# Low-rank branches of a hybrid DiT block: inner weights folded into the in-projection columns on the chip

## Chip, cores and metric

One core of a Trainium2 chip runs the whole program in one launch. The metric is the device time of one execution in microseconds (us). All matrix products are float32 made of three float32r passes: each operand is split into a high part (rounded to float32r) and a low part (what is left), and a product is low x high + high x low + high x high.

## The reference, cut to what matters

The input has 1024 latent tokens ("x") and 256 context tokens ("c"), 1024 wide. An even layer is followed by an odd one. In the odd layer the normed tokens h are multiplied by `in_o`; its first 512 columns give u. u goes through a token shift and then through small inner weights: two of rank 32 for the decay, two of rank 32 for the rate, one of width 96 for the gate:

```python
def token_shift_mix(z, mu):
    zp = jnp.pad(z, ((0, 0), (1, 1), (0, 0)))
    nb = 0.5 * (zp[:, :-2] + zp[:, 2:])
    return z + (nb - z) * mu
...
uw, ua, ugt = (token_shift_mix(u, mu[i]) for i in (3, 4, 5))
g = jax.nn.sigmoid(ugt @ g1) @ g2
tanh(uw @ w1[d]) @ w2[d]        # decay, d = 0, 1
(ua @ a1[d]) @ a2[d]            # rate, d = 0, 1
```

The shift is linear, so the token's own share is u times ((1 - mu) * l1) and its neighbours' share is u times (mu/2 * l1), where l1 = [w1[0], w1[1], a1[0], a1[1], g1] is 512 x 224. u itself is used for nothing else.

## The kernel before, in words

Tokens lie along the free axis, channels on the partitions. A token block is 512 x-tokens (`XB`, two of them) or the 256 context tokens (`CB`). A dense product (`dense`, L294 to L306) goes by output tiles of 128 channels and by token blocks: 24 matmuls (8 channel tiles of the input by three passes) into one of four PSUM banks (`d`), which a consumer then empties.

The order of every engine's instructions is the order in which the code is written. Weights come through `wstream` (L236): one raw buffer `wr` takes a 512 KB tile by a DMA of SyncE, ScalarE casts it to the high half `wh` (L267), GpSimd subtracts to the low half `wl` (L268), and only then may the next tile be loaded to `wr`. SyncE issues its DMAs in the order of the code, and one that has to wait holds back all behind it.

The stretch around the change, in order:

1. The even layer's output projection, tiles m = 0 to 7 of `out_e` (weights 24 to 31 of the stream). For m = 0 to 3 all three token blocks, for m = 4 to 7 x0 and c (first pass), then x1 for m = 4 to 7 (second pass). `fin` (L789) empties the bank on VectorE into the residual `x2x`/`x2c`, ScalarE squares it (L798), GpSimd adds it to `accx`/`accc` (L799). During m = 3 the weights `w2` (tile `rows`) become `WS`: a ScalarE cast (L823) and a VectorE subtraction (L824).
2. The norm of each token block (`norm1`): a ones-matmul (L312) of the sums, an inverse root, and `norm_apply` (L391 to L410) by channel tile over VectorE, ScalarE and GpSimd. Block x0 is done beside the second pass, c after it, x1 beside the next step.
3. u for 4 tiles (weights 32 to 35) and all blocks: 4 x 3 products of 24 matmuls, each emptied by a cast on ScalarE (L847) and a subtraction on VectorE (L848). In between `lora_weights` (L890) makes l1 times (1 - mu) and l1 times mu/2: 24 small VectorE products (L901), two casts, two GpSimd subtractions.
4. `stage1` in `odd_in` (L935 to L960): u by the own and by the neighbour weights, 12 matmuls each, for the 128 decay and rate columns (tile 0, all blocks) and the 96 gate columns padded to 128 (tile 1, x blocks). The neighbours' result `LB` is added shifted to `LA` by GpSimd (L957) and VectorE (L958).
5. The gate's second product (L1393), the projections of k, v and r (L1018) and everything after.

From step 5 on both kernels hold the same instructions in the same order on every engine.

Of the kernel before, what the change touches and what calls it, by code (L numbers as in the profile page):

```python
# [8 lines left out]
F32 = mybir.dt.float32  # L9
F32R = mybir.dt.float32r  # L10
# [169 lines left out]
class Kern:  # L180
# [56 lines left out]
    def wstream(self):  # L237
# [4 lines left out]
        order += [A["in_o"][m] for m in range(4)]  # L242
# [16 lines left out]
        def load(i):  # L259
            raws[i] = self.wfirst = self.wp.tile([128, 8, 128], F32, tag="wr", name="wr")  # L260
            self.wload(raws[i], order[i] if i < n else rest[0])

        def split(i):
            p = self.extra.get(i) or (self.wp, self.wpb)[(n - i) % 2]
# [5 lines left out]
        self.load, self.after = load, None  # L270
# [152 lines left out]
    def layer_even(self, es):  # L423
# [339 lines left out]
        self.WS = self.s_lpw.enter_context(tc.tile_pool(name="lpw", bufs=1)).tile([96, 4, DB], F32R, name="WS")  # L763
        s_x1 = ExitStack()
# [6 lines left out]
        rp0 = s_x0.enter_context(tc.tile_pool(name="rp0", bufs=1))  # L771
        xn, accs, store = {}, {}, []

        def fetch_x(m):
            for s, c0, n in BLK:
                x = (rp1 if c0 else rp0).tile([128, n], F32, tag=f"x2{s}{m}", name=f"x2{s}{m}")
# [8 lines left out]
        def fin(m):  # L785
            def f(s, c0, n, ps):
# [6 lines left out]
                if m == 0:  # L793
                    accs[s, c0] = (rp1 if c0 else rp0).tile([128, n], F32, tag=f"acc{s}", name=f"acc{s}")
# [16 lines left out]
        rows = rp0.tile([96, 4, DB], F32, name="rows")  # L811
        for i in range(3):
            nc.sync.dma_start(out=rows[32 * i:32 * i + 32], in_=A["w2"].rearrange("(g p) n -> p g n", p=32))
        ws = {}
        for m in range(8):
# [6 lines left out]
            if m == 3:  # L822
                nc.scalar.copy(self.WS, rows)  # L823
                nc.vector.tensor_tensor(out=self.WS[32:64], in0=rows[32:64], in1=self.WS[32:64].bitcast(F32), op=ALU.subtract)  # L824
        for m in range(4, 8):
# [6 lines left out]
            if m == 6:  # L832
                w = [next(self.wit)]
# [6 lines left out]
        self.s_up = ExitStack()  # L840
        up = self.s_up.enter_context(tc.tile_pool(name="up", bufs=1))
        self.U = U = [[up.tile([128, TT], F32R, name=f"u{b}{k}") for k in range(4)] for b in range(2)]

        def ue(k):
            def f(src, c0, n, ps):
                o = c0 + (0 if src == "x" else T)
                nc.scalar.copy(U[0][k][:, o:o + n], ps)  # L847
                nc.vector.tensor_tensor(out=U[1][k][:, o:o + n], in0=ps, in1=U[0][k][:, o:o + n].bitcast(F32), op=ALU.subtract)  # L848
            return f
        w.append(next(self.wit))  # L850
        n = 0
        for _ in self.dense(w[0], rhs, XB[:1], ue(0)):
            n += 1
            if n == 18:
                norm = norm1(XB[1])
                next(norm)
        for k, blocks in ((1, XB[:1]), (0, CB), (1, CB), (2, XB[:1] + CB), (0, second), (1, second), (2, second)):
            if k == len(w):
                w.append(next(self.wit))
            if blocks is second and k == 0:  # L860
                list(norm)
            for _ in self.dense(w[k], rhs, blocks, ue(k)):
                n += 1
                if n % self.PN1 == 0:
                    next(norm, None)
            if blocks is second and k == 0:
                s_x1.close()
                self.lora_weights()
        for _ in self.dense(next(self.wit), rhs, BLK, ue(3)):
            pass  # L870
        s_wq.close()
        for k in range(8):
# [16 lines left out]
    def lora_weights(self):  # L889

        tc, nc, A, hmu, omu = self.tc, self.nc, self.A, self.hmu, self.omu
        up = self.s_up.enter_context(tc.tile_pool(name="ul", bufs=1))
        l1 = up.tile([128, 4, 224], F32, name="l1")
        nc.sync.dma_start(out=l1, in_=A["l1"])
        self.LS = LS = []
        for i, mcol in ((0, omu), (1, hmu)):
            lw = up.tile([128, 4, 256], F32, tag="lw", name="lw")
            nc.gpsimd.memset(lw, 0.0)
            for k in range(4):
                for mi, c0, n in ((3, 0, 64), (4, 64, 64), (5, 128, 96)):  # L900
# [1532 lines left out]
```

## Time and profile before

| | us |
|---|---|
| median of the runs | 1514.9 (1507.59 to 1519.34, 3 runs) |
| the profiled execution | 1519.35 |
| its span in the trace | 1517.6 |
| TensorE busy / VectorE / GpSimd / ScalarE | 1366.9 / 987.0 / 679.3 / 639.3 |
| mean granted TensorE clock, share of full | 0.957 |

The span is what the trace covers; 1.75 us lie around it. A busy TensorE is not TensorE at its peak: what counts for a change is how far apart its matmuls start, and where it stands still.

### The profile page before, as it was taken

The numbers are of one execution on the slowest core, as the hardware profiler recorded it, in microseconds if no ns is written. First come the engines' busy times: TensorE is split into PE (matmuls) and PEld (weight loads), VectorE is DVE, ScalarE is ACT, GpSimd is POOL, SyncE is SP. The second block draws the span as 40 slices with busy tenths as digits, with TensorE's granted clock in tenths as the row PEclk, the third lists the DMA queues.
The fourth block names the chain that finished last, engine by engine and source line by source line (L and its number), as shares of the span: only waits on it lengthen the run. The fifth ranks groups of instructions, "written<-read, shape, count | busy, mean of one in ns | idle before, by whom it ended". The sixth has DMA issues, their size and how long they took to land.

```text
span 1517.6 us, 32067 instructions
## 1 busy us (share of the span) xinstructions
PE 1366.9 (90%) x12820; PEld 1074.3 (71%) x12820; DVE 987.0 (65%) x1679; ACT 639.3 (42%) x1259; POOL 679.3 (45%) x943
## 2 busy tenths in 40 slices
PE   6799999999999999898799887698998888887996
PEld 1478888888888778676677666576776666765675
DVE  3745655436711651269999973688668788678756
ACT  2551212121312543456566431243546554566634
POOL 1344535457545441135554540766564665433003
PEclk9999999999999999999899998898999999888998
DMA  8424544453154211536667687555656666755323
GB/s 267 157 81 147 166 156 170 152 167 139 49 170 142 77 41 33 149 101 198 197 196 221 199 277 189 144 135 148 178 138 167 186 163 152 248 167 143 119 81 111
DMA packets 163941, 232.30 MB, mean 153 GB/s; under 512 B 26352, under 2 KB 119920, under 8 KB 163664
## 3 DMA queue, kind: packets, MB, share of 16 engines
q1 hardware_dynamic: 162496, 228.68, 49.9%
q8 instruction: 101, 1.65, 0.5%
q10 hardware_dynamic: 1296, 1.57, 0.3%
q14 instruction: 48, 0.39, 0.1%
HBM read 164.93 MB, written 63.31 MB: 150 GB/s over the span
## 4 chain that ended last, share of the span: by engine, by line
PE 55%; DVE 20%; DMA 8%; issue 5%; POOL 5%; ACT 5%; SPq 2%; DVEq 0%; ACTq 0%; POOLq 0%
PE d L302 28%; PE d L1970 5%; PE d L1018 4%; PE d L2112 3%; PE sc L1534 2%; PE d L946 2%; POOL tmp L1434 2%; POOL X L1435 2%; DMA Bc<-ED 1%; DVE acc L1991 1%; PE pa L1751 1%; PE d L2317 1%; DMA ad<-in_ada_e 1%; PE pa L1756 1%; PE pa L1775 1%
## 5 line engine op out<-in xcount | busy, mean ns | idle before, releaser
L302 PE MATMUL d<-sx,wh 128*128 128x512 f32 x1152 | 361.7, 395 | 3.0 <-DVE sx L528 1.9
L302 PEld LDWEIGHTS d<-sx,wh 128*128 128x128 f32 x1152 | 217.3, 189 | 53.9 <-DVE sx L528 2.4
L302 PE MATMUL d<-sx,wl 128*128 128x512 f32 x576 | 230.1, 399 | 4.5 <-DVE u L848 2.7
L1434 POOL TENSOR_TENSOR tmp<-X,Bc 128x120 f32<-128x120 f32 (+2 forms) x300 | 124.4, 415 | 148.5 <-DMA Bc<-ED 126.2
L268 POOL TENSOR_TENSOR wl<-wr,wh 128x1024 fp32r<-128x1024 f32 x37 | 94.0, 2540 | 190.6 <-ACT wh L267 181.1
L1018 PE MATMUL d<-sx,wh 128*128 128x512 f32 x512 | 162.7, 399 | 0.0
L1970 PE MATMUL d<-sx,wh 128*128 128x512 f32 x384 | 138.4, 431 | 0.0
L1435 POOL TENSOR_TENSOR X<-X,tmp 128x120 f32<-128x120 f32 (+2 forms) x300 | 122.8, 409 | 23.5
L302 PEld LDWEIGHTS d<-sx,wl 128*128 128x128 f32 x576 | 109.0, 189 | 29.6 <-issue 3.3
L629 DVE SCALAR_TENSOR_TENSOR junk<-wra,cb 128x1024 bf16<-128x1024 f32 x56 | 101.1, 1805 | 30.3 <-DMA wra<-in_ada_o 17.5
L1018 PEld LDWEIGHTS d<-sx,wh 128*128 128x128 f32 x512 | 98.7, 193 | 22.1 <-issue 2.4
L1018 PE MATMUL d<-sx,wl 128*128 128x512 f32 x256 | 111.4, 435 | 0.0
L302 PE MATMUL d<-sc,wh 128*128 128x256 f32 x576 | 104.1, 281 | 0.0
L302 PEld LDWEIGHTS d<-sc,wh 128*128 128x128 f32 x576 | 88.8, 190 | 1.4
L1991 DVE SCALAR_TENSOR_TENSOR acc<-hc,vec,acc 128x960 f32<-128x960 f32 (+14 forms) x120 | 88.0, 761 | 1.0
L267 ACT CAST wh<-wr 128x1024 fp32r<-128x1024 f32 x37 | 38.7, 1045 | 112.3 <-PE d L302 82.8
L1970 PEld LDWEIGHTS d<-sx,wh 128*128 128x128 f32 x384 | 73.8, 199 | 16.4
L1970 PE MATMUL d<-sx,wl 128*128 128x512 f32 x192 | 82.7, 430 | 2.7 <-POOL wl L1944 2.7
L302 PE MATMUL d<-sc,wl 128*128 128x256 f32 x288 | 81.0, 281 | 0.0
L1224 POOL TENSOR_TENSOR kd<-kd,Z 128x512 f32<-128x512 f32 x20 | 29.9, 1497 | 75.5 <-DVE kd L1220 75.5
L1534 PE MATMUL sc<-w,bk 64*128 64x128 f32 (+1 forms) x640 | 51.5, 302 | 8.1 <-DMA bk<-BKD 8.1
L1018 PEld LDWEIGHTS d<-sx,wl 128*128 128x128 f32 x256 | 49.3, 193 | 11.6 <-issue 1.9
(382 smaller groups left out, 2889.2 us busy)
## 6 DMA issues: line engine op xcount, KB each, us to landing
wr<-in_in_o SPq DMA_DIRECT2D x32, 512.0 KB
wr<-in_in_e SPq DMA_DIRECT2D x24, 512.0 KB
wra<-in_ada_o SPq DMA_DIRECT2D x24, 512.0 KB
BKD<-bk SPq DMA_DIRECT2D x40, 256.0 KB
BTD<-X SPq DMA_DIRECT2D x20, 512.0 KB
bk<-BKD SPq DMA_DIRECT2D x40, 256.0 KB
Bc<-ED SPq DMA_DIRECT2D x20, 512.0 KB
bkt<-BTD SPq DMA_DIRECT2D x40, 256.0 KB
```

The source lines that it names most:

```text
L267: self.nc.scalar.copy(hi, raw)
L268: self.nc.gpsimd.tensor_tensor(out=lo, in0=raw, in1=hi.bitcast(F32), op=ALU.subtract)
L302: self.nc.tensor.matmul(ps[:, :n], lhsT=w[a][:, k, :], rhs=rhs(src, k, b, c0, n), start=(i == 0), stop=(i == len(seq) - 1))
L629: nc.vector.scalar_tensor_tensor(out=junk, in0=w, scalar=1.0, in1=cb[:, s, :], op0=ALU.mult, op1=ALU.mult, accum_out=dst[:, s:s + 1])
L946: nc.tensor.matmul(ps[:, :n], lhsT=LS[which][a][:, k, 128 * mt:128 * mt + 128], rhs=U[b][k][:, o:o + n], start=(i == 0), stop=(i == len(se ...
L1018: nc.tensor.matmul(ps, lhsT=w[a][:, k, :], rhs=rhs(s, k, b, c0, m), start=(q == 0), stop=(q == len(seq) - 1))
L1434: g.tensor_tensor(out=t, in0=X[:, :, j:j + 1].to_broadcast([128, 8, m]), in1=B[:, j, :, j + 1:16] if j < 8 else B2[:, j - 8, :, j - 7:8], ...
L1435: g.tensor_tensor(out=X[:, :, j + 1:16], in0=X[:, :, j + 1:16], in1=t, op=ALU.add)
L1534: nc.tensor.matmul(ps[h][:, d, i, h:h + 1] if ctx else ps[h][:, d, i], lhsT=bk[R[h], c, d, i], rhs=w[R[h], c, d, sl, i, :], start=True, st ...
L1970: nc.tensor.matmul(ps, lhsT=wt(a, k), rhs=rhs("x", k, b, c0, 512), start=(i == 0), stop=(i == len(seq) - 1))
L1991: nc.vector.scalar_tensor_tensor(out=acc[:, o], in0=hc[:, q], scalar=w, in1=acc[:, o], op0=ALU.mult, op1=ALU.add)
L2112: nc.tensor.matmul(ps, lhsT=wt(a, at), rhs=ysrc(k, b, c0), start=(i == 0), stop=(i == len(seq) - 1))
```

## The change

u is no longer computed. The chip multiplies the in-projection columns of u by the two sets of inner weights first: M = in_o[:, :512] times [(1 - mu) l1, mu/2 l1], 1024 x 448, and then multiplies the tokens h by M. For that:

- The four tiles of the stream that held in-projection columns (weights 32 to 35) are read from a transposed copy `in_oT` of the same numbers, so that u's channels lie on the partitions. `in_oT` is laid out on the host beside the other weights.
- `LA` (the results of both tiles) and `LB` (one neighbour buffer) get a place for the whole stretch, and are used before as landing places: `w2` is loaded to `LA`, l1 to `LB`. Both loads move from the start of the output projection to m = 2.
- `lora_weights` moves to m = 4 of the first pass, behind `WS`. Each of its 24 pieces is now a product (high half) and a scalar_tensor_tensor (low half), both on VectorE.
- Weight 34 is loaded to `LB` as soon as l1 has been read from there, by a DMA written in front of the fetch of the residual for m = 6. Weight 35 is loaded and split early as well, so that all four are there when M starts.
- M is made in two halves of four channel tiles, each 48 matmuls of 448 columns into all four banks `d`, emptied by four casts (ScalarE) and four subtractions (VectorE). In half 1 the four weights are the outer loop, in half 2 the inner one. The norm of c is written in front of half 1, the start of the norm of x1 between the halves.
- `branch` multiplies the tokens by M: 8 channel tiles x 3 passes for (tile, own or neighbour) and block, in the order x0 (4 products), c (2), x1 (4). Tile 1 is 96 wide, no longer padded.
- Context and x0 residual tiles get pools apart (`rpc`, `rp0`).

The core of the diff:

```diff
-        order += [A["in_o"][m] for m in range(4)]
+        order += [A["in_oT"][m] for m in range(4)]
...
+        self.LA = LA = la.tile([128, 2, TT], F32, name="LA")
+        LB = [la.tile([128, TT + 3], F32, name="LB")]
...
-            if m == 3:
+            if m == 2:
+                nc.sync.dma_start(out=l1, in_=A["l1"])
+                for i in range(3):
+                    nc.sync.dma_start(out=rows[32 * i:32 * i + 32], in_=A["w2"].rearrange("(g p) n -> p g n", p=32))
+            if m == 4:
                 nc.scalar.copy(self.WS, rows)
                 nc.vector.tensor_tensor(out=self.WS[32:64], in0=rows[32:64], in1=self.WS[32:64].bitcast(F32), op=ALU.subtract)
+                LW = self.lora_weights(lwp, l1)
+
+                self.raws[34] = LB[0][:, 0:1024].rearrange("p (a n) -> p a n", a=8)
+                self.wload(self.raws[34], self.order[34])
...
-            if m == 6:
-                w = [next(self.wit)]
+            if m == 4:
+                self.split(34)
+            else:
+                w.append(next(self.wit))
+            if m == 5:
+                self.load(35)
+            elif m == 6:
+                self.split(35)
+        self.after()
+        self.after = None
+        w.append(self.ready[35])
         keep()
         list(norm1(first[1]))
...
+        M = [up.tile([128, 8, 448], F32R, name=f"M{b}") for b in range(2)]
+        for hf in range(2):
+            sums = [self.psd.tile([128, 512], F32, tag="d", name="d")[:, :448] for _ in range(4)]
+            for m, q in ([(m, q) for m in range(4) for q in range(4)], [(m, q) for q in range(4) for m in range(4)])[hf]:
+                for e, (a, b) in enumerate(((1, 0), (0, 1), (0, 0))):
+                    nc.tensor.matmul(sums[q], lhsT=w[m][a][:, 4 * hf + q, :], rhs=LW[b][:, m, :], start=(m + e == 0), stop=(m + e == 5))
+            for q, ps in enumerate(sums):
+                hi, lo = (M[b][:, 4 * hf + q, :] for b in range(2))
+                nc.scalar.copy(hi, ps)
+                nc.vector.tensor_tensor(out=lo, in0=ps, in1=hi.bitcast(F32), op=ALU.subtract)
+            if hf == 0:
                 norm = norm1(XB[1])
                 next(norm)
...
+            seq = [(k, a, b) for k in range(KD) for a, b in ((1, 0), (0, 1), (0, 0))]
+            for i, (k, a, b) in enumerate(seq):
+                nc.tensor.matmul(ps, lhsT=M[a][:, k, o:o + p], rhs=rhs(s, k, b, c0, n), start=(i == 0), stop=(i == len(seq) - 1))
...
+        for b, mts in ((XB[0], (1, 0)), (CB[0], (0,))):
+            for mt in mts:
+                for q in (1, 0):
+                    for _ in branch(mt, q, b):
...
+                    nc.vector.tensor_scalar(out=h, in0=l1[:, k, c0:c0 + n], scalar1=m, scalar2=None, op0=ALU.mult)
+                    nc.vector.scalar_tensor_tensor(out=l, in0=l1[:, k, c0:c0 + n], scalar=m, in1=h.bitcast(F32), op0=ALU.mult, op1=ALU.subtract)
```

Three places show how instructions move. First SyncE's queue in the last part of the first pass, before: `wr_3462` is weight 31, the last of `out_e`, and `x2x6` the residual for m = 6.

```order
L294 DMA wr_3391<-in_out_e 128x1024
L783 DMA XR_83<-x2x3_3152 128x512
L777 DMA x2x6_3427<-in_xT 128x512
L777 DMA x2x6_3429<-in_xT 128x512
L777 DMA x2c6_3431<-in_ctxT 128x256
L294 DMA wr_3462<-in_out_e 128x1024
```

The same place now, with `wr_3524` for weight 31:

```order
L298 DMA wr_3400<-in_out_e 128x1024
L796 DMA XR_83<-x2x3_3159 128x512
L298 DMA LB_2936<-in_in_oT 128x1024
L790 DMA x2x6_3489<-in_xT 128x512
L790 DMA x2x6_3491<-in_xT 128x512
L790 DMA x2c6_3493<-in_ctxT 128x256
L298 DMA wr_3524<-in_out_e 128x1024
```

The load of weight 34 to `LB` stands in front of the residual for m = 6 and of weight 31.

Second VectorE at the same time, now; `x2c4` is the last bank emptied for m = 4, `x2x5` the first for m = 5, and between the two parts 42 more rows alternate in the same way.

```order
L802 SCALAR_TENSOR_TENSOR x2c4_3268<-d_3402,mode_115,x2c4_3268 128x256
L841 TENSOR_TENSOR WS_2928<-LA_2935,WS_2928 32x2048
L966 TENSOR_SCALAR LH_3434<-LB_2936,omu_100 128x64
L967 SCALAR_TENSOR_TENSOR LL_3435<-LB_2936,omu_100,LH_3434 128x64
...
L966 TENSOR_SCALAR LH_3434<-LB_2936,hmu_99 128x64
L967 SCALAR_TENSOR_TENSOR LL_3435<-LB_2936,hmu_99,LH_3434 128x64
L966 TENSOR_SCALAR LH_3434<-LB_2936,hmu_99 128x96
L967 SCALAR_TENSOR_TENSOR LL_3435<-LB_2936,hmu_99,LH_3434 128x96
L802 SCALAR_TENSOR_TENSOR x2x5_3365<-d_3495,mode_115,x2x5_3365 128x512
```

Before, `x2x5` followed `x2c4` directly, and `WS` stood one bank earlier; 48 small instructions on `LB` are new here.

Third GpSimd at the end of the second pass, before: the sums for m = 4 to 7 and, as `wl_3760`, the split of weight 33.

```order
L799 TENSOR_TENSOR accx_3045<-accx_3045,sq_3698 128x512
L799 TENSOR_TENSOR accx_3045<-accx_3045,sq_3727 128x512
L799 TENSOR_TENSOR accx_3045<-accx_3045,sq_3756 128x512
L268 TENSOR_TENSOR wl_3760<-wr_3598,wh_3759 128x1024
L799 TENSOR_TENSOR accx_3045<-accx_3045,sq_3789 128x512
L398 TENSOR_TENSOR sc11_136<-x2c1_2959,sc10_135 128x256
```

Now, with the splits of weights 34 (`wl_3764`), 33 (`wl_3797`) and 35 (`wl_3832`):

```order
L812 TENSOR_TENSOR accx_3052<-accx_3052,sq_3760 128x512
L272 TENSOR_TENSOR wl_3764<-LB_2936,wh_3763 128x1024
L812 TENSOR_TENSOR accx_3052<-accx_3052,sq_3793 128x512
L272 TENSOR_TENSOR wl_3797<-wr_3660,wh_3796 128x1024
L812 TENSOR_TENSOR accx_3052<-accx_3052,sq_3828 128x512
L272 TENSOR_TENSOR wl_3832<-wr_3800,wh_3831 128x1024
L812 TENSOR_TENSOR accx_3052<-accx_3052,sq_3861 128x512
L402 TENSOR_TENSOR sc11_136<-x2c1_2966,sc10_135 128x256
```

Two more splits stand among the sums, in front of the norm of c (`sc11`).

## Rows read from the trace of the kernel before

**Rows 1.** The page: busy time by engine, and the chain that ended last.
```profile
PE 1366.9 (90%) x12820; PEld 1074.3 (71%) x12820; DVE 987.0 (65%) x1679; ACT 639.3 (42%) x1259; POOL 679.3 (45%) x943
...
PE 55%; DVE 20%; DMA 8%; issue 5%; POOL 5%; ACT 5%; SPq 2%; DVEq 0%; ACTq 0%; POOLq 0%
```
**Rows 2.** Timeline of TensorE, end of the first pass: start us, us, what.
```profile
471.18 0.39 PE L302 MATMUL d<-sx,wl 128*128 128x512 f32 x1
...
476.78 0.28 PE L302 MATMUL d<-sc,wl 128*128 128x256 f32 x1
...
479.65 0.40 PE L302 MATMUL d<-sx,wl 128*128 128x512 f32 x1
...
488.12 0.40 PE L302 MATMUL d<-sx,wl 128*128 128x512 f32 x1
```
**Rows 3.** Timeline of TensorE, u and stage1; brackets: idle before, and releaser.
```profile
519.98 0.58 PE L302 MATMUL d<-sx,wl 128*128 128x512 f32 x1
...
541.12 0.77 PE L302 MATMUL d<-sx,wl 128*128 128x512 f32 x1 [2.66 <-DVE u L848]
...
544.78 0.40 PE L302 MATMUL d<-sx,wl 128*128 128x512 f32 x1
...
582.91 0.47 PE L946 MATMUL d<-u,LL 128*128 128x512 f32 x1 [0.97 <-POOL LB L939]
...
607.66 1.02 PE L1393 MATMUL d<-LA,g 96*128 96x512 f32 x2
```
**Rows 4.** Stretches: us, busy PE, PEld, DVE, ACT, POOL (instructions), granted clock, DMA share, GB/s.
```profile
472.00:474.00 2.00, 2.00 (x11) 1.58 (x10) 0.00 (x0) 0.38 (x1) 0.94 (x2) 1.00 0.90 219
474.00:476.00 2.00, 2.00 (x10) 1.63 (x9) 0.00 (x0) 0.94 (x1) 0.00 (x0) 1.00 1.03 398
540.00:545.00 5.00, 3.88 (x10) 3.11 (x11) 4.59 (x6) 3.52 (x7) 1.66 (x1) 0.66 0.00 0
```
**Rows 5.** Timeline of VectorE: WS, the last bank of m = 4.
```profile
466.40 2.28 DVE L824 TENSOR_TENSOR WS<-rows,WS 32x2048 fp32r<-32x2048 f32 x1 [2.56 <-ACT WS L823]
...
471.38 0.48 DVE L789 SCALAR_TENSOR_TENSOR x2c<-d,mode,x2c 128x256 f32<-128x256 f32 x1 [1.92 <-PE d L302]
```
**Rows 6.** Line 901 by itself: duration ns min/median/max, first and last start.
```profile
L901 DVE TENSOR_SCALAR lw<-l,omu x12: 247/248/264, 561.4 to 563.3; 128x64 f32<-128x64 f32 x8, 128x96 f32<-128x96 f32 x4
```
**Rows 7.** Timeline of ScalarE: WS, squares, casts of weights, start of c's norm.
```profile
464.47 1.90 ACT L823 CAST WS<-rows 96x2048 fp32r<-96x2048 f32 x1
...
471.96 0.42 ACT L798 ACTIVATE sq<-x2c 128x256 f32<-128x256 f32 x1 [1.77 <-DVE x2c L789]
...
482.30 1.05 ACT L267 CAST wh<-wr 128x1024 fp32r<-128x1024 f32 x1 [1.46 <-DMA wr<-in_out_e]
...
521.33 0.46 ACT L376 ACTIVATE rs<-a,cstt 128x256 f32<-128x256 f32 x1
```
**Rows 8.** Timeline of SyncE's queue: issues at m = 6 of the first pass.
```profile
478.61 0.33 SPq L294 DMA_DIRECT2D wr<-in_out_e  x1
...
479.46 0.95 SPq L777 DMA_DIRECT2D x2x<-in_xT  x2
480.46 0.50 SPq L777 DMA_DIRECT2D x2c<-in_ctxT  x1
```
**Rows 9.** Timeline of GpSimd: x0's norm, sums, a weight's split, end of c's norm.
```profile
506.52 1.87 POOL L398 TENSOR_TENSOR sx<-x2x,sx 128x512 fp32r<-128x512 f32 x1 [7.93 <-ACT sx L406]
...
516.68 4.05 POOL L799 TENSOR_TENSOR accx<-accx,sq 128x512 f32<-128x512 f32 x3 [0.31 <-ACT sq L798]
520.69 2.41 POOL L268 TENSOR_TENSOR wl<-wr,wh 128x1024 fp32r<-128x1024 f32 x1
...
532.11 0.74 POOL L398 TENSOR_TENSOR sc<-x2c,sc 128x256 fp32r<-128x256 f32 x1 [0.51 <-ACT sc L406]
```
**Rows 10.** Timeline of VectorE: two of the norm's subtractions (L400).
```profile
505.17 0.75 DVE L400 SCALAR_TENSOR_TENSOR sx<-x2x,modo,sx 128x512 fp32r<-128x512 f32 x1
...
507.38 1.57 DVE L400 SCALAR_TENSOR_TENSOR sx<-x2x,modo,sx 128x512 fp32r<-128x512 f32 x1
```

More of the change, by code (lines that the diff above doesn't have):

```diff
@@ L268, in split @@
             self.nc.gpsimd.tensor_tensor(out=lo, in0=raw, in1=hi.bitcast(F32), op=ALU.subtract)
-        self.load, self.after = load, None
+        self.load, self.split, self.after = load, split, None
         load(0)
@@ L810, in layer_even @@
         fetch_x(0)
-        rows = rp0.tile([96, 4, DB], F32, name="rows")
-        for i in range(3):
-            nc.sync.dma_start(out=rows[32 * i:32 * i + 32], in_=A["w2"].rearrange("(g p) n -> p g n", p=32))
+        rows = LA[0:96].rearrange("p a t -> p (a t)")[:, 0:4 * DB].rearrange("p (g n) -> p g n", g=4)
+        l1 = LB[0][:, 0:896].rearrange("p (k n) -> p k n", k=4)
         ws = {}
@@ L855, in layer_even @@
                 norm = norm1(XB[1])
                 next(norm)
[L857 to L868, printed above, removed]
@@ L869, in layer_even, with branch @@
-        for _ in self.dense(next(self.wit), rhs, BLK, ue(3)):
-            pass
+        next(self.wit)
+        LB.append(lwp.tile([128, TT + 3], F32, tag="lwh", name="LB1"))
+        for b in LB:
+            for c in (0, T + 1, TT + 2):
+                nc.gpsimd.memset(b[:, c:c + 1], 0.0)
+        def branch(mt, q, b):
+            s, c0, n = b
+            p, o = (128, 96)[mt], 224 * q + 128 * mt
+            ps = self.psd.tile([128, 512], F32, tag="d", name="d")[0:p, :n]
+            seq = [(k, a, b) for k in range(KD) for a, b in ((1, 0), (0, 1), (0, 0))]
+            for i, (k, a, b) in enumerate(seq):
+                nc.tensor.matmul(ps, lhsT=M[a][:, k, o:o + p], rhs=rhs(s, k, b, c0, n), start=(i == 0), stop=(i == len(seq) - 1))
+                yield 1
+            z = c0 + (0 if s == "x" else T)
+            if q:
+                z += 1 if s == "x" else 2
+                nc.scalar.copy(LB[mt][0:p, z:z + n], ps)
+            else:
+                nc.scalar.copy(LA[0:p, mt, z:z + n], ps)
+            if self.after:
+                self.after()
+                self.after = None
@@ L871, in layer_even @@
+        list(norm)
+        s_x1.close()
+        for mt in (1, 0):
+            for q in (1, 0):
+                for _ in branch(mt, q, XB[1]):
+                    pass
+            shifted(mt)
+            if mt:
+                Hg = LA[0:96, 1, 0:T]
+                nc.scalar.activation(out=Hg, in_=Hg, func=AF.Tanh, scale=0.5)
+                nc.vector.tensor_scalar(out=Hg, in0=Hg, scalar1=0.5, scalar2=0.5, op0=ALU.mult, op1=ALU.add)
+        s_up.close()
         s_wq.close()
+        s_lw.close()
```

100 lines of the change are left out of this document (36 added, 64 removed).

## The prediction

> **What bounds the kernel now.** I read the page first: TensorE is busy for 90% of the span, and the chain that ended last runs through it for 55% [rows 1]. So a shorter stretch of matmuls shortens the program, provided that nothing TensorE waits for becomes later. Both kernels hold the same instructions in the same order from the gate's second product on, so the question is only when TensorE gets there. I then read TensorE's timeline from the end of the first pass to that point. A block of 24 matmuls of 512 columns takes 476.78 - 471.18 = 5.60 us, one of 256 columns 479.65 - 476.78 = 2.87 us [rows 2]. u starts at 519.98 and the gate's product at 607.66 [rows 3], 87.7 us later. In that stretch TensorE hardly rests: it waits 2.66 us for a bank that VectorE empties late, and 0.97 us at the change of PSUM pools [rows 3]. In the five microseconds around the first wait the granted clock averages 0.66, against 1.00 in the other two stretches shown [rows 4], so part of it ran on the lower level, 1.2 GHz. Last I followed the other queues (SyncE, VectorE, ScalarE, GpSimd), because the change puts new work and a new wait in each.
>
> **Matmuls.** Before: u is 8 blocks of 512 and 4 of 256; stage1 is 96 matmuls of 512, as many as 4 blocks, and 24 of 256, 1 block. 12 x 5.60 + 5 x 2.87 = 81.6 us. After: branch is 8 blocks of 512 and 2 of 256. M is 96 matmuls of 448 columns, 4 blocks; no row has that width, and it lies between 2.87 and 5.60. The line through both gives 2.87 + 192/256 x 2.73 = 4.92 us. 8 x 5.60 + 2 x 2.87 + 4 x 4.92 = 70.2 us. **-11.3 us.** (With M's blocks at 5.60, their upper end, -8.6.)
>
> **Old waits.** Between 541.12 and 544.78 nine matmuls started [rows 3], 3.66 us for what takes 9 x 0.233 = 2.10 at the full clock: 1.56 us lost to the lower level. The wait of 2.66 and this loss go, since u's banks go: **-4.2 us**. The wait at the change of pools moves behind branch and stays.
>
> **Weight 31 comes late.** This is the first new wait, and the change does not show it as one. Weight 34 may not land in `LB` before l1 has been read there, so its DMA waits for the last of the 48 small VectorE instructions. SyncE issues in order, and behind that DMA stand the residual for m = 6 and weight 31, which m = 7 multiplies by from 488.12 on [rows 2]. The steps: the last bank of m = 4 is empty at 471.86 [rows 5]; its square ends at 472.38; the cast of WS takes 1.90, to 474.28 [rows 7]; the subtraction of WS 2.28, to 476.6 [rows 5]. A product of that size lasts 248 ns and, where nothing holds it, starts 0.17 us after the one before [rows 6]. Here the second of each pair reads what the first wrote, so it starts after the first's end. I take 0.28 for the first and 0.19 for the second, 0.47 a pair, an estimate near the full duration: 24 pairs are 11.3 us, to 487.9. (If the pairs overlap like the rows, 24 x 0.35 = 8.4; with no overlap, 24 x 0.50 = 12.) From weight 34's issue to weight 31's, SyncE needs some 0.4 + 1.0 + 0.5 = 1.9 us [rows 8]: weight 31 is issued at 489.8 instead of 478.61. Alone it landed 3.7 us later, at 482.30 [rows 7, 8]. Now 1.15 MB are on the way in front of it; at the best rate of the rows, 398 GB/s [rows 4], these and its own 0.52 MB take 4.2 us from about 490, so it lands near 494.4. The cast of 1.05 [rows 7] and the split of 2.41 [rows 9] end at 498.0. TensorE stands still from 488.12: **+9.9 us**. The ends: with 8.4 for the pairs and a landing after 3.7 it is 6.2. Upwards, GpSimd splits weight 30 just then, and VectorE and GpSimd hold each other up: beside a GpSimd instruction of 1.87 us [rows 9] a VectorE subtraction took 1.57 instead of 0.75 [rows 10]. One such loss of 0.8, or one of a whole split, 2.4, and DMAs at 219 GB/s [rows 4] (3.4 more) make 15.8. After the wait the clock is low for a while, as above: **+1.5**. The banks cost nothing meanwhile: m = 5's are emptied by 489, and m = 6 needs two others.
>
> On the loss between VectorE and GpSimd the Trainium skill (SBUF — State Buffer, section "SBUF: two separate sides") goes further than the row: a VectorE instruction with two SBUF inputs, or in a two-port mode, and a GpSimd instruction exclude each other for the whole instruction. By that rule VectorE waits for all of weight 30's split, and the term is 9.9 + 2.4 = 12.3 instead of 9.9. The rows show only a collision with a shorter instruction, so I keep 9.9.
>
> **M waits three times.** Call E the end of the second pass, where u starts before (519.98 [rows 3]). GpSimd now does sum, split 34, sum, split 33: from 516.68 [rows 9] that is 2 x 1.35 + 2 x 2.41 = 7.5 us, to E + 4.2; half 1 reaches weight 33 after its first quarter, at E + 2.5, and waits 1.7. Only then is `wr` free for weight 35: landing 3.7 later, cast 1.05, split 2.41, E + 11.5; half 1 gets there at E + 9.1 and waits 2.4. It ends near E + 14.0. All four banks are then full, and their casts stand on ScalarE behind c's norm, which stands behind the cast of weight 35 and one more square (E + 9.7). Before, that norm took from 521.33 [rows 7] to 532.85 [rows 9], 11.5 us: to E + 21.2. Cast and subtraction of the first bank take some 1.2 us; half 2 starts at E + 22.4 instead of E + 14.0. The waits: 1.7 + 2.4 + 8.4 = **+12.5 us**, and **+1.5** for the clock behind the longest. From below: 6, if c's norm keeps to its bare durations and only the banks are waited for. From above: 15 and two such losses of the clock. The rest of x1's norm fits beside branch on x0 and c, 4 x 5.60 + 2 x 2.87 = 28 us.
>
> **Free edits.** The padding of tile 1 costs columns of weights only, and the matmuls go by tokens: nothing. The earlier loads of l1 and `w2` have three output tiles to land in. The zero fill, casts and splits of l1 that go lay beside u's matmuls: nothing.
>
> **Sum.** -11.3 - 4.2 + 9.9 + 1.5 + 12.5 + 1.5 = +9.9 us. On the profiled execution that is 1519.35 + 10 = 1529. That execution was 4.4 us above the median of the runs, so against the median I say 1514.9 + 9.9 = 1525. With all low ends, -15.5 + 6.2 + 1.5 + 6 + 1.5 = -0.3; with all high ones, and M's blocks at 5.60, -12.8 + 15.8 + 1.5 + 15 + 3 = +22.5.
>
> **Rivals.**
> *Weight 31 is in time.* If SyncE does not stand at weight 34 (the pairs quicker than any row, or the wait met earlier), the terms 9.9 and 1.5 go: 9.9 - 11.4 = -1.5, 1513. Against it: the order of SyncE's queue and 48 instructions behind WS. For it: I have no row of these pairs. Part of it counts here too, anything between -10 and 0.
> *The whole gain arrives.* Both new waits are hidden: -15.5, 1499. Against it speak both chains above; for it only that each rests on estimated overlaps.
> *The clock stays low through M.* Three waits in some 30 us, one long stop just before. If the clock does not come back between them, M's 96 matmuls run at 3.66/2.10 = 1.74 times the time: 19.7 becomes 34.3, +14.6 in place of 1.5, and the sum is +23: 1538. It decides as soon as half 1 and half 2 both run on the lower level. For it: one wait of 2.66 was enough to bring the level down [rows 3, 4]. Against it: it was back within four microseconds. The Trainium skill (TensorE: Matmul & The Clock Gate, section "HAM oscillation — how this bites in real kernels") tells of a kernel in which every group of matmuls starts on the lower level because each is preceded by a wait; the row shows one wait alone, and so decides neither way.
>
> **How the numbers follow.** The forecast has 0.55, weight 31 in time 0.25, the low clock through M 0.15, the whole gain 0.05. A measurement of this kernel can tell about 1% (15 us) from no change. The forecast and the first rival lie within it: same 0.80. The third is beyond: slower 0.15. The second sits at the edge: faster 0.05. The forecast's own range goes from about 0 to +15, 1515 to 1530; to hold 8 in 10 with the first rival's lower part, the upper ends, and runs that differ by several microseconds, the range is 1508 to 1534.
>
> **What would show it.** In the profile of the changed kernel: the DMA `LB<-in_in_oT` issued near 488 and weight 31 near 490; a wait of TensorE for `wl` by GpSimd near 488 to 498, in front of m = 7; M's rows 0.2 us apart; waits of some 2, 2 and 8 us inside M, the last for VectorE's `M`; granted clock below 1 behind the longest waits; everything from the gate's product on as before, only shifted. The prediction is wrong if m = 7 starts on time, if half 2 follows half 1 without a wait, or if the shift at the gate's product is not the change of the whole.

## The result, and the profile after

The changed kernel takes 1527.2 us (median of 21 runs, 1520.8 to 1537.7) beside 1514.9 us for the kernel before (21 runs on the same chip): ratio 1.0078, 95% interval 1.0057 to 1.0099. That is 12.4 us or 0.8% slower: within the 1% that the prediction called no change, and inside its range. The profiled execution took 1529.83 us with a span of 1528.0; the span of before was 1517.6. A ratio, here and in the table below, is taken over the runs within 1.5% of the fastest run of their kernel; this leaves out few, but a run of l1_apart that took 4354.9 us, and five of the twelve runs of full, where a single run of 1486.7 us sets the bar.

The page, busy time by engine and the chain that ended last, now:

```profile
PE 1360.9 (89%) x12748; PEld 1065.2 (70%) x12748; DVE 999.0 (65%) x1699; ACT 634.7 (42%) x1253; POOL 670.2 (44%) x939
...
PE 29%; DVE 14%; issue 6%; DMA 6%; POOL 3%; ACT 3%; SPq 1%; DVEq 0%; ACTq 0%; POOLq 0%
```

TensorE is busy 6 us less than in [rows 1], and the program is longer: matmuls were saved, and waits took more than they gave. The second line does not show that. Its shares add up to 62% of the span, because the chain is followed back only to 561.50, inside M; so its 29% for TensorE cannot be set beside the 55% of [rows 1]. TensorE's timeline shows the waits; first the end of the first pass (start, duration, what; in brackets idle time before and its releaser), which answers to [rows 2]:

```profile
480.22 0.28 PE L306 MATMUL d<-sc,wl 128*128 128x256 f32 x1
...
488.68 0.28 PE L306 MATMUL d<-sc,wl 128*128 128x256 f32 x1
...
505.57 0.79 PE L306 MATMUL d<-sx,wl 128*128 128x512 f32 x1 [13.93 <-POOL wl L272]
...
513.56 0.28 PE L306 MATMUL d<-sc,wl 128*128 128x256 f32 x1
```

This execution is 3.44 us late already in the c block of m = 5 (480.22 against 476.78 [rows 2]); it has been since 73 us, in the loads at the start, which the change does not touch. So stretches are compared, not clock times. From that c block to the gate's product it was 607.66 - 476.78 = 130.9 us [rows 2, 3] and is 624.06 - 480.22 = 143.8: **+13.0**, about the change of the whole. The first part of it is the 13.93 in front of m = 7, which was due 2.87 us behind the c block of m = 6 (488.68). That block of 24 then takes 513.56 - 505.57 = 7.99 instead of 5.60: 2.4 lost to the lower clock. The second part is in M (answers to [rows 3]):

```profile
539.76 0.55 PE L878 MATMUL d<-LH,wl 128*128 128x448 f32 x1
540.16 0.37 PE L878 MATMUL d<-LL,wh 128*128 128x448 f32 x1
...
542.18 0.37 PE L878 MATMUL d<-LH,wh 128*128 128x448 f32 x1
543.75 0.47 PE L878 MATMUL d<-LH,wl 128*128 128x448 f32 x1 [1.19 <-POOL wl L272]
...
550.57 0.47 PE L878 MATMUL d<-LH,wl 128*128 128x448 f32 x1 [1.72 <-POOL wl L272]
...
561.50 0.74 PE L878 MATMUL d<-LH,wl 128*128 128x448 f32 x1 [7.37 <-DVE M L882]
...
565.03 0.48 PE L878 MATMUL d<-LH,wl 128*128 128x448 f32 x1
565.35 0.36 PE L878 MATMUL d<-LL,wh 128*128 128x448 f32 x1
...
573.10 2.22 PE L899 MATMUL d<-sx,M 128*96 128x512 f32 x9
...
624.06 1.10 PE L1421 MATMUL d<-LA,g 96*128 96x512 f32 x2 [0.72 <-issue]
```

Three waits, 10.3 us in sum; nine matmuls behind the last one take 565.03 - 561.50 = 3.53 instead of 9 x 0.204 = 1.84. From 539.76 to the gate's product it is 84.3 us, 3.4 less than the 87.7 of before [rows 3]: in this stretch, taken by itself, the change won. The granted clock (the number before the DMA share), in five stretches of after, answers to [rows 4]:

```profile
505.00:511.00 6.00, 5.43 (x14) 4.29 (x15) 0.00 (x0) 1.04 (x1) 2.89 (x4) 0.53 0.46 131
511.00:516.00 5.00, 5.00 (x33) 4.50 (x32) 0.75 (x1) 0.63 (x1) 2.61 (x2) 1.00 0.38 104
543.00:545.00 2.00, 1.25 (x6) 1.18 (x7) 0.00 (x0) 0.00 (x0) 1.94 (x2) 1.00 0.13 25
550.00:552.00 2.00, 1.43 (x7) 1.34 (x8) 1.42 (x2) 0.51 (x1) 1.95 (x2) 1.00 0.25 49
561.00:566.00 5.00, 4.50 (x14) 4.06 (x15) 4.08 (x7) 3.03 (x6) 0.00 (x0) 0.57 0.00 0
```

Behind the two long waits TensorE starts on the lower level, 1.2 GHz, and comes back within some 5 us; behind the two short ones it stays at 2.4 GHz.

SyncE's queue, which answers to [rows 8]:

```profile
494.22 0.33 SPq L298 DMA_DIRECT2D LB<-in_in_oT  x1
494.60 0.90 SPq L790 DMA_DIRECT2D x2x<-in_xT  x2
495.55 0.43 SPq L790 DMA_DIRECT2D x2c<-in_ctxT  x1
496.09 0.36 SPq L298 DMA_DIRECT2D wr<-in_out_e  x1
```

Weight 34's DMA was issued at 494.22, and weight 31's, the last row, 1.87 us behind it; before it went out at 478.61 [rows 8]. What weight 34 waited for is on VectorE (answers to [rows 5, 6]):

```profile
477.70 2.28 DVE L841 TENSOR_TENSOR WS<-LA,WS 32x2048 fp32r<-32x2048 f32 x1 [2.39 <-ACT WS L840]
480.01 2.29 DVE L966 TENSOR_SCALAR LH<-LB,omu 128x64 fp32r<-128x64 f32 x1
482.34 0.28 DVE L967 SCALAR_TENSOR_TENSOR LL<-LB,omu,LH 128x64 fp32r<-128x64 f32 x1
482.54 0.25 DVE L966 TENSOR_SCALAR LH<-LB,omu 128x64 fp32r<-128x64 f32 x1
...
493.88 0.32 DVE L967 SCALAR_TENSOR_TENSOR LL<-LB,hmu,LH 128x96 fp32r<-128x96 f32 x1
494.11 0.75 DVE L802 SCALAR_TENSOR_TENSOR x2x<-d,mode,x2x 128x512 f32<-128x512 f32 x1
```

The 48 small instructions end at 494.2, and only behind them is m = 5's first bank emptied (L802). GpSimd's split of weight 30 beside the first of them, and ScalarE's casts (answer to [rows 7, 9]):

```profile
478.63 3.61 POOL L272 TENSOR_TENSOR wl<-wr,wh 128x1024 fp32r<-128x1024 f32 x1 [2.00 <-ACT wh L271]
```

```profile
494.95 0.63 ACT L811 ACTIVATE sq<-x2x 128x512 f32<-128x512 f32 x1 [16.39 <-DVE x2x L802]
495.49 0.40 ACT L811 ACTIVATE sq<-x2c 128x256 f32<-128x256 f32 x1
502.05 1.04 ACT L271 CAST wh<-wr 128x1024 fp32r<-128x1024 f32 x1 [6.16 <-DMA wr<-in_out_e]
...
547.03 1.05 ACT L271 CAST wh<-wr 128x1024 fp32r<-128x1024 f32 x1 [7.72 <-DMA wr<-in_in_oT]
547.99 0.63 ACT L811 ACTIVATE sq<-x2x 128x512 f32<-128x512 f32 x1
548.52 0.46 ACT L380 ACTIVATE rs<-a,cstt 128x256 f32<-128x256 f32 x1
...
560.25 1.84 ACT L881 CAST M<-d 128x448 fp32r<-128x448 f32 x4 [0.83 <-POOL sc L402]
```

Two chains are to be read here. Weight 31 lands at 502.05, and its cast and split end at 505.5, where m = 7 starts. And in M, ScalarE stands 7.72 us idle for weight 35 (547.03); c's norm begins only behind that (548.52), and M's four casts behind the norm (560.25).

### The profile page after: what moved, and what is told of

Read it like the earlier page. It is cut to its first block, busy times and chain, and to the rows that moved or that the text cites. A ratio compares the mean times of both kernels' runs of the same rounds, so it can differ in the third digit from the quotient of the medians.

```text
span 1528.0 us, 31916 instructions
## 1 busy us (share of the span) xinstructions
PE 1360.9 (89%) x12748; PEld 1065.2 (70%) x12748; DVE 999.0 (65%) x1699; ACT 634.7 (42%) x1253; POOL 670.2 (44%) x939
## 4 chain that ended last, share of the span: by engine, by line
PE 29%; DVE 14%; issue 6%; DMA 6%; POOL 3%; ACT 3%; SPq 1%; DVEq 0%; ACTq 0%; POOLq 0%
PE d L1999 6%; PE d L1046 4%; PE d L2141 4%; PE sc L1563 2%; PE pa L1785 1%; POOL tmp L1463 1%; PE pa L1780 1%; POOL X L1464 1%; PE d L899 1%; PE pa L1804 1%; PE po L1775 1%; DMA Bc<-ED 1%; PE d L2346 1%; PE po L1798 1%; PE d L878 1%
## 5 line engine op out<-in xcount | busy, mean ns | idle before, releaser
L306 PE MATMUL d<-sx,wh 128*128 128x512 f32 x1024 | 323.1, 397 | 2.5 <-DVE sx L532 1.4
L306 PEld LDWEIGHTS d<-sx,wh 128*128 128x128 f32 x1024 | 194.3, 190 | 47.7 <-POOL sx L402 1.8
L306 PE MATMUL d<-sx,wl 128*128 128x512 f32 x512 | 204.9, 400 | 15.8 <-POOL wl L272 15.2
L1463 POOL TENSOR_TENSOR tmp<-X,Bc 128x120 f32<-128x120 f32 (+2 forms) x300 | 120.2, 401 | 148.7 <-DMA Bc<-ED 126.2
L1046 PE MATMUL d<-sx,wh 128*128 128x512 f32 x512 | 162.8, 400 | 0.0
L1999 PE MATMUL d<-sx,wh 128*128 128x512 f32 x384 | 137.1, 427 | 0.0
L306 PEld LDWEIGHTS d<-sx,wl 128*128 128x128 f32 x512 | 97.4, 190 | 38.2 <-POOL wl L272 15.8
L633 DVE SCALAR_TENSOR_TENSOR junk<-wra,cb 128x1024 bf16<-128x1024 f32 x56 | 102.4, 1828 | 28.6 <-DMA wra<-in_ada_o 15.8
L1046 PEld LDWEIGHTS d<-sx,wh 128*128 128x128 f32 x512 | 98.4, 192 | 21.7 <-issue 2.2
L1046 PE MATMUL d<-sx,wl 128*128 128x512 f32 x256 | 110.8, 433 | 0.0
L306 PE MATMUL d<-sc,wh 128*128 128x256 f32 x512 | 92.4, 281 | 0.0
L1999 PEld LDWEIGHTS d<-sx,wh 128*128 128x128 f32 x384 | 73.0, 197 | 16.1 <-issue 0.2
L1999 PE MATMUL d<-sx,wl 128*128 128x512 f32 x192 | 81.8, 426 | 2.7 <-POOL wl L1973 2.7
L306 PEld LDWEIGHTS d<-sc,wh 128*128 128x128 f32 x512 | 78.8, 189 | 1.3
L306 PE MATMUL d<-sc,wl 128*128 128x256 f32 x256 | 71.9, 281 | 0.0
L1563 PEld LDWEIGHTS sc<-w,bk 64*128 64x128 f32 x640 | 43.5, 201 | 20.4 <-issue 18.0
```

Of the source, the lines that this page charges most:

```text
L306: self.nc.tensor.matmul(ps[:, :n], lhsT=w[a][:, k, :], rhs=rhs(src, k, b, c0, n), start=(i == 0), stop=(i == len(seq) - 1))
L633: nc.vector.scalar_tensor_tensor(out=junk, in0=w, scalar=1.0, in1=cb[:, s, :], op0=ALU.mult, op1=ALU.mult, accum_out=dst[:, s:s + 1])
L1046: nc.tensor.matmul(ps, lhsT=w[a][:, k, :], rhs=rhs(s, k, b, c0, m), start=(q == 0), stop=(q == len(seq) - 1))
L1463: g.tensor_tensor(out=t, in0=X[:, :, j:j + 1].to_broadcast([128, 8, m]), in1=B[:, j, :, j + 1:16] if j < 8 else B2[:, j - 8, :, j - 7:8], ...
L1563: nc.tensor.matmul(ps[h][:, d, i, h:h + 1] if ctx else ps[h][:, d, i], lhsT=bk[R[h], c, d, i], rhs=w[R[h], c, d, sl, i, :], start=True, st ...
L1999: nc.tensor.matmul(ps, lhsT=wt(a, k), rhs=rhs("x", k, b, c0, 512), start=(i == 0), stop=(i == len(seq) - 1))
```

## The experiments

The table puts all of them together. "Ratio" is to runs of the kernel before on the same chip, with its interval. "Stretch" is from the c block of m = 5 to the gate's product in the profiled execution (before: 130.9); the last two columns are TensorE's wait in front of m = 7 and its waits inside M, in us. An execution takes 903.4 to 916.0 us from the gate's product to its end in the ten profiles, though the instructions there are the same; so the stretch, though read from one execution each, is less blurred than the time.

| | ratio | stretch | m = 7 | M |
|---|---|---|---|---|
| changed kernel | 1.0078 (1.0057 to 1.0099) | +13.0 | 13.9 | 10.3 |
| w34_behind | 1.0051 (1.0024 to 1.0079) | +6.6 | 8.3 | 10.3 |
| l1_apart | 1.0058 (1.0021 to 1.0094) | +7.4 | 8.3 | 10.3 |
| cnorm_early | 1.0035 (1.0011 to 1.0058) | +7.3 | 13.8 | 5.1 |
| both | 0.9999 (0.9962 to 1.0036) | +0.6 | 6.5 | 5.0 |
| cast_ahead | 1.0024 (0.9993 to 1.0056) | +4.4 | 5.4 | 10.2 |
| lora_spread | 0.9998 (0.9969 to 1.0027) | -1.8 | 0 | 10.1 |
| full | 0.9916 (0.988 to 0.9952) | -7.0 | 0 | 5.8 |
| joined | 1.0007 (0.9978 to 1.0036) | +1.2 | 0 | 12.9 |

### Weight 34's load moved behind weight 31's (w34_behind)

```diff
                 LW = self.lora_weights(lwp, l1)
-
+            if m == 6:
                 self.raws[34] = LB[0][:, 0:1024].rearrange("p (a n) -> p a n", a=8)
                 self.wload(self.raws[34], self.order[34])
```

> The changed kernel with one edit: the load of weight 34 is written behind weight 31's, at the end of m = 6 of the first pass. In the changed kernel TensorE waits 13.93 us in front of m = 7 and then loses some 2.4 us to the lower clock. Theory A (SyncE stands at weight 34's DMA and holds weight 31 back): weight 31 is issued as soon as m = 5's first products are done, near 482, and is split before 491. What is left in front of m = 7 is the next thing late: VectorE empties m = 5's first bank only behind the 48 small instructions, at 494.9, where m = 7 wants it at 491.6, so a wait of about 3 us and part of the clock loss. The time falls by 11 to 14 us against the changed kernel, to about 1514. Theory B (the 48 instructions themselves are what m = 7 waits for, through the banks, and SyncE's queue only looks late): the wait in front of m = 7 stays above 10 us and the time moves by less than 4.

Neither theory's number came. The wait fell by 5.6 us, to 8.32, still for weight 31's split, and by the ratios the time fell by some 4 us, not by 11 to 14. TensorE and ScalarE of this run:

```profile
497.65 0.79 PE L306 MATMUL d<-sx,wl 128*128 128x512 f32 x1 [8.32 <-POOL wl L272]
```

```profile
492.64 0.63 ACT L811 ACTIVATE sq<-x2x 128x512 f32<-128x512 f32 x1 [16.39 <-DVE x2x L802]
493.18 0.40 ACT L811 ACTIVATE sq<-x2c 128x256 f32<-128x256 f32 x1
493.48 1.03 ACT L271 CAST wh<-wr 128x1024 fp32r<-128x1024 f32 x1
```

Weight 31 was issued at 479.96, but its cast stood in ScalarE's queue behind m = 5's squares, and these waited for VectorE, which was busy with the small instructions. So SyncE's hold was real, and behind it lay a second chain of which neither I nor the rival had thought.

### The same without moving the load: l1 in tiles of its own (l1_apart)

```diff
-        l1 = LB[0][:, 0:896].rearrange("p (k n) -> p k n", k=4)
+        l1 = [rq.tile([128, 512], F32, tag=t, name=t)[:, :448].rearrange("p (k n) -> p k n", k=2) for t in ("ms", "rs")]
...
-                nc.sync.dma_start(out=l1, in_=A["l1"])
+                for i in range(2):
+                    nc.sync.dma_start(out=l1[i], in_=A["l1"][:, 2 * i:2 * i + 2])
```

> The changed kernel with one edit: l1 is loaded to two scratch tiles of its own in place of LB, so that weight 34's DMA stands at the same place in SyncE's queue but has nothing to wait for. Theory A (the wait of that DMA holds back those behind it): weight 34 is issued near 475, weight 31 near 482, and the wait in front of m = 7 falls from 13.93 to about 3 us (the banks), the time by 11 to 14 us, as when the load is moved. Theory C (what is late is traffic: 0.5 MB more in front of weight 31): weight 31 lands later by a microsecond or two wherever weight 34 stands before it, so that moving the load helps and this edit does not; the wait stays above 10 us.

SyncE and TensorE of this run:

```profile
467.58 0.43 SPq L298 DMA_DIRECT2D LB<-in_in_oT  x1
...
477.26 0.33 SPq L298 DMA_DIRECT2D wr<-in_out_e  x1
```

```profile
494.95 0.79 PE L306 MATMUL d<-sx,wl 128*128 128x512 f32 x1 [8.33 <-POOL wl L272]
```

Weight 34 goes out without waiting, and the wait in front of m = 7 is 8.33 us, that of w34_behind to 0.01. So it was the waiting of the DMA in front of weight 31 that cost the 5.6 us, not the 0.5 MB that it moves: theory C's wait of over 10 us is out. Theory A's 3 us did not come either, for the same second chain as in w34_behind. Whether weight 31 lands a microsecond later for the traffic is not shown here, since its cast waits for the squares in any case.

### Weight 31's cast in front of m = 5's squares (cast_ahead)

On top of w34_behind, in the function that empties the banks:

```diff
             def f(s, c0, n, ps):
+                if m == 5 and s == "x" and not c0:
+                    self.after()
+                    self.after = None
+                    self.split(31)
```

> As w34_behind (weight 34's load behind weight 31's), and in addition the cast and split of weight 31 are written in front of the square of m = 5's first block, where they stood behind m = 5's two squares. In w34_behind TensorE still waits 8.32 us in front of m = 7: weight 31's cast came at 493.48, right behind those squares (492.64, 493.18), which wait for VectorE's 48 small instructions. Theory D (a second chain: VectorE's block holds the squares, and ScalarE's queue holds weight 31's cast behind them): the cast runs when the weight has landed, near 484, and the split ends near 488; what is left in front of m = 7 is m = 5's first bank, emptied at 492.6 where m = 7 wants it at 489.3, so 3 us, or 5 to 6 if the split of weight 31 now holds VectorE up for its whole 2.4 us as weight 30's did. The wait is then for VectorE and not for the split. Rival E (weight 31 itself lands late, and the squares are in front of the cast by chance): the wait stays near 8 and is for GpSimd's split.

Theory D, with the higher of its two numbers. TensorE, VectorE and GpSimd of this run:

```profile
495.70 0.77 PE L306 MATMUL d<-sx,wl 128*128 128x512 f32 x1 [5.36 <-DVE x2x L806]
```

```profile
486.04 2.30 DVE L971 SCALAR_TENSOR_TENSOR LL<-LB,omu,LH 128x64 fp32r<-128x64 f32 x1
488.27 0.26 DVE L970 TENSOR_SCALAR LH<-LB,omu 128x96 fp32r<-128x96 f32 x1
...
494.81 0.74 DVE L806 SCALAR_TENSOR_TENSOR x2x<-d,mode,x2x 128x512 f32<-128x512 f32 x1
```

```profile
485.84 2.42 POOL L272 TENSOR_TENSOR wl<-wr,wh 128x1024 fp32r<-128x1024 f32 x1 [4.89 <-ACT wh L271]
```

The releaser is now VectorE, which empties the bank. One small instruction took 2.30 us instead of 0.28 and ended within 0.1 us of the split beside it. So three chains lay over one another in front of m = 7, all of them behind VectorE's block: SyncE's queue (13.9), ScalarE's queue (8.3), the bank (5.4).

### The block cut in three (lora_spread)

On top of w34_behind, with `lora_weights` made a generator that yields behind each pair:

```diff
-            if m == 4:
+            if m == 3:
                 nc.scalar.copy(self.WS, rows)
...
-                LW = self.lora_weights(lwp, l1)
+                lora = self.lora_weights(lwp, l1)
+                LW = next(lora)
+            if 4 <= m < 7:
+                for _ in range(8):
+                    next(lora, None)
```

> The changed kernel with weight 34's load behind weight 31's, WS made at m = 3 as in the kernel before, and the 24 pairs of small VectorE instructions in three pieces of 8 pairs, behind m = 4, 5 and 6. By theory D VectorE now never stands more than some 4 to 6 us (8 x 0.5, and one split of GpSimd beside it) between two banks that come 5.6 us apart, so the squares, weight 31's cast and the banks are in time: wait in front of m = 7 below 1.5 us, against 13.93 in the changed kernel and 8.32 with the load alone moved; no low clock behind it; TensorE reaches the gate's product 15 us sooner than in the changed kernel, counted from the start of m = 6. Time near 1512 to 1515 (before: 1518 on that chip, 1515 on the first). Rival: the pieces collide with the splits and residual adds of each tile, and a wait of 3 us or more stays in front of m = 6 or 7 or the second pass.

No wait is left in front of m = 7. The stretch is 14.7 us shorter than in the changed kernel (15 expected), and the time is that of the kernel before. Two things changed beside the load: `WS` is made one tile sooner, and the block is cut. How much each gives is not shown apart. A part of the rival came true: x0's norm waits 1.35 us for a sum of GpSimd in the second pass.

### The context norm in front of weight 35's split (cnorm_early)

```diff
             else:
+                if m == 7:
+                    cn = norm1(first[1])
+                    for _ in range(3):
+                        next(cn)
                 w.append(next(self.wit))
             if m == 5:
                 self.load(35)
-            elif m == 6:
-                self.split(35)
...
-        list(norm1(first[1]))
+        list(cn)
```

> The changed kernel with one edit: the norm of the context tokens is begun in front of the split of weight 35 and not behind it, so that ScalarE does not stand idle for weight 35's landing (540.4 to 547.0) with the norm and the four casts of M behind it. Theory A (the second half of M waits for banks whose casts stand behind that norm): the wait of 7.37 us inside M falls to about 1, and with it most of the 1.7 us lost to the lower clock behind it; weight 35's split stays within 1 us of where it was; the time falls by 6 to 9 us against the changed kernel, to about 1520. Theory B (the norm is not what the casts wait for, or the split of weight 35 moves as much as the norm): the two last waits in M together stay at 8 us or more and the time moves by less than 2.

The wait for the banks is gone, so it was the norm that the casts waited for. But weight 35's split came 2.2 us later (counted from the start of M), and half 1 waits for it instead:

```profile
543.83 0.47 PE L880 MATMUL d<-LH,wl 128*128 128x448 f32 x1 [1.18 <-POOL wl L272]
...
552.87 0.74 PE L880 MATMUL d<-LH,wl 128*128 128x448 f32 x1 [3.88 <-POOL wl L272]
```

M's waits fall from 10.3 to 5.1, the stretch by 5.6: somewhat under the 6 to 9 of theory A, and far from B's 2.

### Both, and the small instructions in front of WS (both)

The edits of w34_behind and cnorm_early, and in m = 4:

```diff
+                LW = self.lora_weights(lwp, l1)
                 nc.scalar.copy(self.WS, rows)
                 nc.vector.tensor_tensor(out=self.WS[32:64], in0=rows[32:64], in1=self.WS[32:64].bitcast(F32), op=ALU.subtract)
-                LW = self.lora_weights(lwp, l1)
```

> The changed kernel with weight 34's load behind weight 31's, the context norm begun in front of weight 35's split, and the 48 small instructions written in front of the making of WS (so they start some 4 us sooner and the first bank of m = 5 is emptied near 490, in time for m = 7). If my terms add up, no wait is left in front of m = 7 (-13.9 - 2.4) and about 1 us in front of the second half of M (-6.4 - 1.5): 24 us under the changed kernel, 1503, and 12 under the kernel before, which is the gain of the matmuls and of the old waits (-15.5) less the two short waits inside M (3). Rival: the gain does not come through to the end because what follows the gate's product has slack or other waits of its own; then TensorE reaches that product 24 us sooner and the time falls by much less.

The stretch fell by 12.4 us instead of 24. The second chain (unknown when this was written) still left 6.5 us in front of m = 7, the block behind it took 7.72 us instead of 5.60, and M waits 5.0 us where some 4 were expected. The time is that of the kernel before, by the ratios 12 us under the changed kernel's: what was saved up to the gate's product came through to the end, so the rival falls.

### A version that beats both (full)

lora_spread and cnorm_early together, with weight 33 split in front of 34:

```diff
-            if m == 4:
-                self.split(34)
-            else:
+            if m == 7:
+                cn = norm1(first[1])
...
+            if m != 6:
                 w.append(next(self.wit))
-            if m == 5:
+            if m == 4:
                 self.load(35)
```

(33 and 34 also exchange the pools that they are split into.)

> lora_spread, and in addition: the context norm begun in front of weight 35's split (as in cnorm_early), and weight 33 split in front of weight 34 with weight 35's load right behind that. Expected from the rows of cnorm_early: weight 33 is there before half 1 reaches it (no wait of 1.2), weight 35's cast stands behind three steps of the norm, so the third wait (3.9 us, for weight 35's split) stays or grows by the 1.2, and half 2 follows without a wait: M's waits 4 to 5 us against 10.3 in the changed kernel. Counted from the start of m = 6 to the gate's product some 21 us under the changed kernel and 8 under the kernel before: about 1507.

Over all its twelve runs the median is 1507.9 us beside the 1514.4 of the kernel before, 6.5 us less, and the mean 1506.6 beside 1514.5 (ratio 0.995, 0.991 to 0.998 at two standard errors). That agrees with the 1507 expected and with the stretch, which is 7.0 us under that of before and 19.9 under the changed kernel's (21 expected). The ratio of 0.9916 in the table, over seven of the runs, would make it 13 us and is too favourable. The two waits that it still has inside M, 5.8 us where 4 to 5 were expected:

```profile
534.98 0.74 PE L882 MATMUL d<-LH,wl 128*128 128x448 f32 x1 [5.29 <-POOL wl L272]
...
540.41 0.47 PE L882 MATMUL d<-LH,wl 128*128 128x448 f32 x1 [0.49 <-DVE M L886]
```

### The norm begun still earlier (joined)

As full, with the context norm written behind m = 5 of the second pass, and weight 35's split behind m = 6:

```diff
-            if m == 7:
-                cn = norm1(first[1])
-                for _ in range(3):
-                    next(cn)
...
+            elif m == 5:
+                cn = norm1(first[1])
+                for _ in range(2):
+                    next(cn)
+            elif m == 6:
+                self.split(35)
+                list(cn)
...
-        list(cn)
```

> As full, but the context norm is begun behind m = 5 of the second pass, right behind the x0 norm, and weight 35 is split after two channel tiles of it. If ScalarE and VectorE have the room there (they idle for some 2 and 7 us before the end of the second pass in the changed kernel), weight 35's split ends near where half 1 wants it and the norm ends 3 to 4 us sooner than in cnorm_early: M's waits 2 to 4 us in sum. Rival: the norm then stands in front of the emptying of m = 6 and 7 on VectorE and of their squares, and the sums of x1 and half 1's banks get later by as much; then M's waits are no smaller than in full.

The rival came true:

```profile
530.82 0.74 PE L884 MATMUL d<-LH,wl 128*128 128x448 f32 x1 [5.21 <-DVE x2x L802]
...
540.00 0.74 PE L884 MATMUL d<-LH,wl 128*128 128x448 f32 x1 [7.69 <-DVE x2x L802]
```

M waits 5.21 and 7.69 us, both for VectorE's emptying of m = 6 and 7, which now stands behind steps of the norm. The time is that of the kernel before.

## Why the prediction was right, and where not

The time came out as forecast (1525 against 1527.2), by the mechanisms that it named, with one term too small and one too large. Part of the closeness is luck: weight 31 cost 4.9 us more than forecast, while M's waits cost 2.0 and the matmuls 0.7 less. Of the +13.0 us some 1.1 is in none of the terms.

**Matmuls, right.** M's matmuls start 0.202 us apart (540.16 to 542.18 for ten), a block of 24 takes 4.85 (4.92 estimated); branch, from 573.10 to the idle before 624.06, takes 50.2 (50.5). Together -12.0 where I had -11.3. **Old waits, right:** the 2.66 and its low clock are gone, and 0.72 takes the place of the 0.97.

**Weight 31 late, right in kind, too small:** 13.9 + 2.4 instead of 9.9 + 1.5. Less the 3.44, the small instructions began at 476.57 (476.6 forecast) and ended at 490.8 instead of 487.9. Of these 2.9 us, 2.0 are the first instruction's wait for the split; the rest is the pairs, whose two instructions do not overlap: 482.34 to 494.20 is 11.86 for 47, 0.50 a pair and not 0.47. From issue to cast weight 31 took 5.96 instead of 4.6. The 1.87 on SyncE, and 3.5 for cast and split, were as forecast. Redone from their own rows, the ends of this term are about 6.0 and 15.7, not 6.2 and 15.8, and the data in front of weight 31 are 1.18 MB, not 1.15; the forecast does not hang on these.

The step at fault is the choice in the sentence on VectorE and GpSimd: I had taken from one row that the two slow each other down a little, and put a whole lost split into the upper bound alone. The Trainium skill (SBUF — State Buffer, section "SBUF: two separate sides") has a VectorE instruction with two SBUF inputs, or in a two-port mode, and a GpSimd instruction exclude each other for the whole instruction. Here the trace agrees: the split of weight 30 (median 2.40) took 3.61, as if its work began only where WS's subtraction ended, at 479.98, and the small instruction behind it ended with the split at 482.3. The trace of before had the same collision, beside the subtraction of WS [rows 5], though none of the rows read for the prediction shows it:

```profile
467.38 3.57 POOL L268 TENSOR_TENSOR wl<-wr,wh 128x1024 fp32r<-128x1024 f32 x1 [1.45 <-ACT wh L267]
```

```profile
468.71 0.75 DVE L789 SCALAR_TENSOR_TENSOR x2x<-d,mode,x2x 128x512 f32<-128x512 f32 x1
```

That split began inside the subtraction and ended 2.27 us behind its end (468.68), while the emptying of a bank beside it took its usual 0.75. With the rule of a whole lost split I had 12.3, nearer than 9.9. What 9.9 lacked is the 2.0 of this wait, the 0.9 of the pairs and the 1.4 of the slower landing, to within 0.3 us.

**M's waits, right in kind and order, too large:** 1.2, 1.7 and 7.4 instead of 1.7, 2.4 and 8.4. The clock cost 1.7 (1.5 forecast). cnorm_early shows the last wait's cause as I had it.

**"The banks cost nothing", and the rival "weight 31 is in time", wrong.** I took m = 5's banks to be empty by 489; the first was empty at 494.86, or 491.4 with the 3.44 taken off, when m = 7 wanted it at 488.1. And I let the terms 9.9 and 1.5 go as soon as SyncE does not stand. The runs show that this takes away 5.6 of the 13.9 us of waiting. The changed kernel hid two more chains behind the first, because the square (on ScalarE, in front of weight 31's cast) and the bank both follow VectorE's block. The forecast of the time was not touched, since the longest of the three sets it; the price of that rival was.

**The other rivals.** The clock did not stay low through M: the two short waits left it at 1.00 (the stretches of 543 and 550 above), and of M's groups behind a wait, only the one behind the longest starts on the lower level. So this trace does not show what the Trainium skill (TensorE: Matmul & The Clock Gate, section "HAM oscillation — how this bites in real kernels") tells of its kernel, where every group starts on the lower level. "The whole gain" was out of reach for the kernel as written; full gets 7.0 of the 15.5 in its stretch, with 5.8 of waits left in M. The shift of the gate's product, +13.0 us in the stretch, is that of the whole, 12.4 between the medians. The two profiled executions by themselves could not show it: from the gate's product on, that of before takes 909.9 us and that of after 903.9.

## What to carry to other kernels

When a wait is found, look for what else stands behind the same late instruction: here one block of small VectorE work fed SyncE's, ScalarE's and TensorE's queues at once, and taking away the wait that the profile named uncovered the next two (13.9, 8.3, 5.4 us) until the block itself was cut to fit between two banks. Fewer matmuls are only worth what the queues that prepare them leave: 12 us of them were won here, and 16 us of new waits in front of m = 7 and 12 in M were paid. A load that may have to wait belongs behind the loads that are wanted sooner.

## What the hardware showed that I had not expected

The VectorE instructions seen beside a split that read only SBUF tiles did not share with it: a VectorE instruction of 0.25 us took 2.29 beside a split, one of 0.28 took 2.30, and a split of 2.40 took 3.61 beside a VectorE subtraction. An emptying of a bank, which reads PSUM, kept its 0.75 beside a split. lora_spread has three more small instructions that took 2.35 to 2.39 us, each beside a split. Of TensorE's waits, those of 1.19 and 1.72 us left the granted clock at 1.00, while behind 2.66 [rows 3, 4], 7.37 and 13.93 it was 0.53 to 0.66 in the stretches shown, and 1.6 to 2.4 us were lost each time, though the waits' lengths differ by five times. Weight 31 took 5.96 us from issue to cast with 1.18 MB issued just in front of it, where it took 3.7 without [rows 7, 8].
